# Weight-stationary blocks in 512-column matmuls: high weights against high and low activations at once, summed when the bank is emptied

## The chip, the cores and the metric

One Trainium2 chip, one of its cores. The metric is the device time of one execution in microseconds; a measurement is the median of several executions. A profiled execution also gives a trace of every instruction, with its start, its duration and what it waited for. The engines are TensorE (PE in the trace; its weight loads PEld), VectorE (DVE), ScalarE (ACT), GpSimd (POOL) and SyncE (SP), which issues the DMAs.

## The reference

Three transformer layers over 256 tokens of width 1024, batch 1, in float32, one after the other:

```
x = first_block(x, ...)      # convolutions + stick-breaking attention, then a feed-forward of 4096
return second_block(x, ...)  # layer 0: retention, gated conv feed-forward of 2816
                             # layer 1: differential attention, gated conv feed-forward of 2816

# the projections are all of this kind, x normalised before and residuals around:
p = h @ w_in                                # 1024 -> 2816 columns, cut into conv parts and q, k, v
x = x + square(relu(h2 @ w_ff1)) @ w_ff2
proj = xn @ a_w_in                          # retention: q, k, v, g
h = xn @ w_up ; hc = causal_conv3(h) ; (silu(hc_g) * hc_u) @ w_down
```

A first conv part goes into the sum as `y_a = a_b * conv3(a_c * a_h)`, a second through a causal convolution of 31 taps, a layer norm and a SiLU (`y_b`), and the attention as `y_c`; `[y_a, y_b, y_c] @ w_out` closes the first mixing.

## The kernel before, in words

Each float32 matrix product is made of float32r matmuls (one pass each) over split numbers: a weight unit of 128 x 1024 is loaded by DMA into `raw`, ACT copies it rounded into `hi`, DVE writes the rest into `lo`; activations are split in the same way into a high and a low half (`sx.hi`, `sx.lo`: eight blocks of 128 channels x 256 tokens). A product is then high x high + high x low + low x high, three matmuls into one PSUM bank (128 x 512 float32; there are eight banks).

There are three ways to walk a product. `wstat` (line 508) keeps 128 x 128 weights in the array and streams the 256 tokens: eight steps over the channels with three matmuls each, on half a bank, and the result has channels on the partitions. `xstat` and `xstat_tokens` keep activations in the array and stream 512 weight columns. `Down` (line 576) does the closing projections in the second way with an accumulator of two banks for each half of the tokens; it takes up the activations `y` one block of 128 channels at a time, and holds back the second token half of the last seven blocks until the first half is done.

The order of the instructions is planned. `Flow` (line 145) runs the kernel's generators against a clock of its own, with a cost for each operation, and hands each engine its operations in the order in which they come up there; each engine then has this order fixed. When several are ready, the lower priority number goes first: CHAIN, ATT, EVAC, SPLIT, IDLE, MAIN (line 236). On DVE and ACT that means attention chains, then the emptying of banks, then weight splits (which run ahead of TensorE by a ring of eight units), and last IDLE, which is the 31-tap convolution `conv_b` of the mix stage (line 719) on DVE. `Slots` hands out banks and buffers, first come first served.

The names that matter: in the mix stage `qk_evac` (833) copies q and k out of a bank, `conv_a` (849) takes three blocks, `MIX_KT` sets that the closing projection takes up blocks 4, 5, 6, 7, 0, 2, 3, 1, of which 2 and 3 come from `conv_b`. In the feed-forward `evac` (933) applies ReLU and square. In retention `rotate` (988) reads two blocks that lie in the two halves of one bank. In the conv stages (two of them, `conv_phase`, 1112) `gate` (1128) reads the gate block and the up block in the halves of one bank, convolves both (three taps: one ACT, two DVE operations each), multiplies and splits; four gates at the start (`early`, 1164) get their blocks by transposes, and `lagged` sets the closing step of block i five blocks behind its up. In the attention stage `evac` (1209) copies q and k.

Of the kernel before, what the change touches and what calls it, by code (L numbers as in the profile page):

```python
# [238 lines left out]
class Acts:  # L239


    def __init__(self, hi, lo):
        self.hi, self.lo = hi, lo
        self.reset()
# [13 lines left out]
def chain_kernel(ctx: ExitStack, tc: tile.TileContext, x_in, wpack, gains, chan, small_rows, consts, out):  # L258
# [153 lines left out]
    ch = cpool.tile([P, NCH], F32, tag="ch", name="ch")  # L412
    sx = Acts(cpool.tile([P, KD, S], F32R, tag="xh", name="xh"), cpool.tile([P, KD, S], F32R, tag="xl", name="xl"))

# [70 lines left out]
    def residual_post(t, acc, ready, g, hg):  # L485
# [20 lines left out]
        return [stt(p, x, h, r, x, ALU.mult, ALU.add) for x, h in zip(xs, hs)]  # L506

    def wstat(dst, w, sx):
        hi, lo = yield from take("ws", w)
        h3 = hi.rearrange("p (k c) -> p k c", k=KD)  # L510
        l3 = lo.rearrange("p (k c) -> p k c", k=KD)
        for k in range(KD):
            if k % 4 == 0:
                yield sx.ready[0][k // 4]
                yield sx.ready[1][k // 4]
            o = pe(MAIN, 358, [
                mm(dst, h3[:, k, :], sx.hi[:, k, :], k == 0, False),
                mm(dst, h3[:, k, :], sx.lo[:, k, :], False, False),
                mm(dst, l3[:, k, :], sx.hi[:, k, :], False, k == KD - 1)])
            yield o.end  # L520
        release(ring, o)
        return o
# [110 lines left out]
    def mix_phase(mp):  # L633
# [199 lines left out]
        def qk_evac(pp, o, dst):  # L833
            yield o
            yield act(EVAC, dst, pp[:, :S], AF.Copy)
            banks.put()

        for i in range(4):
            pr = []
            for what in range(2):  # L840
                pp = yield from banks.get()
                o = yield from wstat(pp[:, :S], "w_in", sx)
                d = yield from qks.get()
                pr.append((d, flow.spawn(qk_evac(pp, o, d))))
            flow.spawn(stick(i, pr))
            if i == V_AFTER:
                yield from xstat("w_in", sx, v_evac)

        def conv_a(c, banks3, o1, o2, o3):
            pc, ph, pb = banks3  # L850
            yield o1
            ac = mp.tile([P, S], F32, tag=f"ac{c}", name=nm("ac"))
            yield act(EVAC, ac, pc[:, :S], AF.Copy)
            banks.put()
            up = mp.tile([P, S + 2], F32, tag=f"up{c}", name=nm("up"))
            nc.gpsimd.memset(up[:, 0:2], 0.0)
            yield o2
            yield tt(EVAC, up[:, 2:], ph[:, :S], ac, ALU.mult)
            banks.put()
            yield consts_in  # L860
            ca = ac
            yield ts(EVAC, ca, up[:, 2:], ch[:, CA0 + 3 * c + 2:CA0 + 3 * c + 3], None, ALU.mult)
            for j in (1, 0):
                yield stt(EVAC, ca, up[:, j:j + S], ch[:, CA0 + 3 * c + j:CA0 + 3 * c + j + 1], ca, ALU.mult, ALU.add)
            yield o3
            yield tt(EVAC, ca, pb[:, :S], ca, ALU.mult)
            banks.put()
            yield from split_to(EVAC, yh[:, c, :], yl[:, c, :], ca)
            flow.fire(y_ready[c])

        for c in range(2):
            trio, ops = [], []
            evs = [Ev() for _ in range(3)]
            pc = yield from banks.get()
            o1 = yield from wstat(pc[:, :S], "w_in", sx)
            ph = yield from banks.get()
            o2 = yield from wstat(ph[:, :S], "w_in", sx)
            pb = yield from banks.get()
            o3 = yield from wstat(pb[:, :S], "w_in", sx)
            flow.spawn(conv_a(c, (pc, ph, pb), o1, o2, o3))  # L880
# [19 lines left out]
    def ff_phase(fp):  # L900
# [32 lines left out]
        def evac(pp, o, y):  # L933
            yield o
            rl = yield from rls.get()
            yield act(EVAC, rl, pp[:, :S], AF.Relu)
            banks.put()
            yield tt(EVAC, rl, rl, rl, ALU.mult)
            yield from split_to(EVAC, y[0], y[1], rl)
            rls.put()  # L940
# [16 lines left out]
        for what, i in lagged(NF, 8):  # L957
            if what == "up":
                pp = yield from banks.get()
                o = yield from wstat(pp[:, :S], w1, sx)  # L960
                y = yield from both.get()
                ys[i] = (y, flow.spawn(evac(pp, o, y)), both)
            else:
                yield from dn.step(*ys.pop(i))
# [8 lines left out]
    def ret_phase(rp):  # L973
# [9 lines left out]
        qs = [Slots(flow, 1, lambda w=w: rp.tile([P, 2, S], F32, tag=f"q{w}", name=nm("q"))) for w in range(2)]  # L983
        rots = Slots(flow, 1, lambda: [rp.tile([P, 2, S], F32, tag=f"rot{c}", name=nm("rot")) for c in "cs"])
        pds = Slots(flow, 1, lambda: [rp.tile([P, 384], d, tag=f"pd{c}", name=nm("pd")) for c, d in (("f", F32), ("h", F32R), ("l", F32R))])
        sgs = slots(rp, 2, [P, 512], F32, "sgl")

        def rotate(pp, o, dst):
            yield o
            for c in cops:  # L990
                yield c
            tcos, tsin = yield from rots.get()
            p3 = pp.rearrange("p (a c) -> p a c", a=2)
            a = tt(EVAC, tcos, p3, cosb.broadcast_to([P, 2, S]), ALU.mult)
            b = tt(EVAC, tsin, p3, sinb.broadcast_to([P, 2, S]), ALU.mult)
            yield a
            yield b
            banks.put()
            a = tt(EVAC, dst[:, 0, :], tcos[:, 0, :], tsin[:, 1, :], ALU.subtract)
            b = tt(EVAC, dst[:, 1, :], tsin[:, 0, :], tcos[:, 1, :], ALU.add)  # L1000
            yield a
            yield b
            rots.put()
# [60 lines left out]
        for h in range(RH):  # L1064
# [30 lines left out]
            for what in range(2):  # L1095
                pp = yield from banks.get()
                yield from wstat(pp[:, 0:S], "a_w_in_2", sx)
                o = yield from wstat(pp[:, S:2 * S], "a_w_in_2", sx)
                d = yield from qs[what].get()
                pr.append((d, flow.spawn(rotate(pp, o, d))))  # L1100
# [11 lines left out]
    def conv_phase(layer, fp, gain_ids, chain_of):  # L1112
# [3 lines left out]
        both = Slots(flow, TAIL + 2, lambda: (fhs.make(), fls.make()))  # L1116
        cvs = Slots(flow, 3, lambda: [fp.tile([P, S], F32, tag=f"cv{c}", name=nm("cv"), bufs=3) for c in range(2)])
        nat = fp.tile([P, 2, D], F32, tag="nat", name="nat")
        n_ready = [[Ev(), Ev()], [Ev(), Ev()]]
# [8 lines left out]
        def gate(pp, o_g, o_u, i, y, nat_i):  # L1128
            cg, cu = yield from cvs.get()
            ps_g, ps_u = pp[:, 0:S], pp[:, S:2 * S]  # L1130
            if nat_i is not None:
                for e in n_ready[0] + n_ready[1]:
                    yield e
                o_g, o_u = [tp(EVAC, [(d[:, t * P:(t + 1) * P], nat[:, t, c0 + nat_i * P:c0 + (nat_i + 1) * P]) for t in range(2)])
                            for d, c0 in ((ps_g, 0), (ps_u, 512))]
            yield o_g
            yield o_u
            a = flow.spawn(conv(EVAC, ps_g, cg, 0, i))
            b = flow.spawn(conv(EVAC, ps_u, cu, 1, i))
            yield a  # L1140
            o = act(EVAC, cg, cg, AF.Silu)
            yield b
            banks.put()
# [27 lines left out]
        for what, i in lagged(NF2, 4):  # L1171
            if what == "up":
                pp = yield from banks.get()
                o_g = yield from wstat(pp[:, 0:S], w_up, sx)
                o_u = yield from wstat(pp[:, S:2 * S], w_up, sx)
                y = yield from both.get()
                ys[i] = (y, flow.spawn(gate(pp, o_g, o_u, i, y, None)), both)
            else:
                yield from dn.step(*ys.pop(i))

    def diff_phase(dp, sb):
# [27 lines left out]
        def evac(pp, o, d, p):  # L1209
            yield o  # L1210
            yield act(p, d, pp[:, :S], AF.Copy)
            banks.put()
# [102 lines left out]
        for h in range(DH):  # L1315
            pr = []
            p = CHAIN + 0.5 if h >= DH - URGENT else ATT
            for what in range(2):
                pp = yield from banks.get()
                o = yield from wstat(pp[:, :S], "w_kv_2" if what == 0 else "b_w_q_2", sx if what == 0 else sb)  # L1320
                d = yield from qks[what].get()
# [21 lines left out]
    def main():  # L1343
# [6 lines left out]
        with tc.tile_pool(name="bresp", bufs=1, reuse_waits="tile") as bp:  # L1350
            sb = Acts(bp.tile([P, KD, S], F32R, tag="bh", name="bh"), bp.tile([P, KD, S], F32R, tag="bl", name="bl"))
            with tc.tile_pool(name="cf0p", bufs=1, reuse_waits="tile") as fp:
# [105 lines left out]
```

## Time and profile before

| | |
|---|---|
| median of 3 runs | 994.86 us (994.24 to 995.26) |
| profiled execution, its own time | 995.56 us |
| its span, first to last instruction | 993.8 us |
| mean granted TensorE clock | 0.998 of full speed |
| TensorE busy | 980.7 us (99%), 6108 matmuls |
| DVE busy | 689.3 us (69%) |
| ACT busy | 562.5 us (57%) |

How to read it: a matmul's row starts when it enters the array, and its modelled end overlaps the next one, so the pace is the distance between starts. All operations are recorded in one helper, so every row says L198, and groups are told apart by their tiles: `bank<-xh,hi` is a matmul that streams high activations against high weights. The 256-column groups are the blocks of `wstat`, the 512-column ones the other two ways. A DVE or ACT row's duration also overlaps its successor a little.

### The profile page before, as it was taken

How to read it: one execution, taken by the hardware profiler on the slowest of the kernel's cores; microseconds unless marked ns; L12 is line 12 of the kernel's file. 1: busy time of each engine (PE TensorE's matmuls, PEld its weight loads, DVE VectorE, ACT ScalarE, POOL GpSimd, SP SyncE). 2: the span in 40 equal slices, each digit the busy share in tenths (PEclk: the TensorE clock that was granted, in tenths of full speed). 3: DMA queues.
4: the chain of work that ended last, by engine and by line, in shares of the span. 5: the costliest groups of instructions: out<-in, count | busy, mean ns of one | idle time of the engine just before them, and what ended most of it. 6: DMA issues, size and time to landing. Idle time of an engine off the chain costs nothing.

```text
span 993.8 us, 15342 instructions
## 1 busy us (share of the span) xinstructions
PE 980.7 (99%) x6108; PEld 876.1 (88%) x6108; DVE 689.3 (69%) x1076; ACT 562.5 (57%) x952; POOL 30.2 (3%) x52
## 2 busy tenths in 40 slices
PE   7999999999999999999999999999999999999997
PEld 5899889999988989988889999997899789999996
DVE  5899775555558756665579666668777579776663
ACT  6654564444446444544567555556677767555551
POOL 1000000000000000000000000001000100000000
PEclk9999999999999999999999999999999999999999
DMA  8744455555436744554366555543733155655531
GB/s 300 257 133 176 179 212 187 195 173 207 171 128 228 264 164 147 178 188 174 123 219 250 185 192 173 209 169 135 266 148 134 54 199 205 236 182 177 184 107 43
DMA packets 28585, 180.14 MB, mean 181 GB/s; under 512 B 3168, under 2 KB 4448, under 8 KB 8672
## 3 DMA queue, kind: packets, MB, share of 16 engines
q1 hardware_dynamic: 28512, 179.14, 50.7%
q8 instruction: 48, 0.79, 0.3%
q14 instruction: 25, 0.20, 0.1%
HBM read 178.08 MB, written 1.05 MB: 180 GB/s over the span
## 4 chain that ended last, share of the span: by engine, by line
PE 92%; DVE 2%; ACT 2%; issue 2%; DMA 1%; POOL 1%; SPq 0%; DVEq 0%; POOLq 0%; ACTq 0%
PE bank L198 92%; ACT junk L198 1%; DVE lo L198 1%; DMA big<-gains 1%; POOL tiny L198 1%; DVE x L198 1%; DVE big L198 0%; ACT hi L198 0%; ACT L198 0%; DVE tiny L198 0%; ACT pe L198 0%; ACT aT L198 0%; DVE xl L198 0%; ACT dyh L198 0%; SPq L198 0%
## 5 line engine op out<-in xcount | busy, mean ns | idle before, releaser
L198 DVE TENSOR_TENSOR lo<-raw,hi 128x1024 fp32r<-128x1024 f32 (+1 forms) x344 | 393.7, 1153 | 129.7 <-ACT hi L198 128.5
L198 ACT ACTIVATE hi<-raw 128x1024 fp32r<-128x1024 f32 (+1 forms) x344 | 341.2, 1003 | 154.6 <-PE bank L198 138.9
L198 PE MATMUL bank<-xh,hi 128*128 128x256 f32 x1072 | 306.1, 286 | 0.0
L198 PE MATMUL bank<-xh,lo 128*128 128x256 f32 x1072 | 303.3, 283 | 0.0
L198 PE MATMUL bank<-xl,hi 128*128 128x256 f32 x1072 | 303.3, 283 | 0.0
L198 PEld LDWEIGHTS bank<-xh,hi 128*128 128x128 f32 x1072 | 205.4, 192 | 3.7 <-issue 1.0
L198 PEld LDWEIGHTS bank<-xl,hi 128*128 128x128 f32 x1072 | 205.4, 192 | 2.6
L198 PEld LDWEIGHTS bank<-xh,lo 128*128 128x128 f32 x1072 | 205.3, 191 | 0.0
L198 PE MATMUL bank<-hi,xh 128*128 128x512 f32 x288 | 114.1, 396 | 0.0
L198 PE MATMUL bank<-lo,xh 128*128 128x512 f32 x288 | 112.4, 390 | 0.2 <-DVE lo L198 0.2
L198 PE MATMUL bank<-hi,xl 128*128 128x512 f32 x288 | 112.5, 391 | 0.0
L198 DVE SCALAR_TENSOR_TENSOR cv<-bank,ch,cv 128x254 f32<-128x254 f32 (+1 forms) x176 | 72.5, 476 | 51.6 <-ACT cv L198 51.4
L198 PE MATMUL bank<-hi,fh 128*128 128x512 f32 x272 | 106.9, 393 | 0.0
L198 PE MATMUL bank<-lo,fh 128*128 128x512 f32 x272 | 106.5, 391 | 0.0
L198 PE MATMUL bank<-hi,fl 128*128 128x512 f32 x272 | 105.8, 389 | 0.0
L198 ACT ACTIVATE cv<-bank,ch 128x256 f32<-128x256 f32 x88 | 44.1, 561 | 61.4 <-PE bank L198 61.4
L198 PEld LDWEIGHTS bank<-hi,xl 128*128 128x128 f32 x288 | 54.0, 188 | 11.8 <-DVE xl L198 0.2
L198 PEld LDWEIGHTS bank<-lo,xh 128*128 128x128 f32 x288 | 54.2, 188 | 11.5 <-DVE lo L198 1.0
L198 PEld LDWEIGHTS bank<-hi,xh 128*128 128x128 f32 x288 | 54.1, 188 | 10.4
L198 PEld LDWEIGHTS bank<-hi,fl 128*128 128x128 f32 x272 | 51.1, 188 | 11.0
L198 PEld LDWEIGHTS bank<-hi,fh 128*128 128x128 f32 x272 | 51.3, 189 | 9.1
L198 PEld LDWEIGHTS bank<-lo,fh 128*128 128x128 f32 x272 | 51.3, 189 | 8.5
(167 smaller groups left out, 1039.8 us busy)
## 6 DMA issues: line engine op xcount, KB each, us to landing
raw<-wpack SPq DMA_DIRECT2D x155, 1024.0 KB, 4.8
big<-gains SPq DMA_DIRECT2D x12, 512.0 KB, 6.9
raw<-wpack SPq DMA_DIRECT2D x12, 512.0 KB, 6.9
x<-x SPq DMA_DIRECT2D x4, 256.0 KB, 6.1
out_dram<-x SPq DMA_DIRECT2D x4, 256.0 KB, 2.2
dec<-consts SPq DMA_DIRECT2D x4, 192.0 KB, 5.0
one<-consts SPq DMA_DIRECT2D x1, 384.0 KB, 6.3
ch<-chan SPq DMA_DIRECT2D x1, 213.5 KB, 5.9
```

What stands on the lines that cost most here:

```text
L198: fn(*a, **k)
```

## The change

The high and the low half of the activations become the two planes of one tile (`both`). In each step of `wstat` the high weights meet both planes in one 512-column matmul, which fills the whole bank: high x high in its first half, high x low in its second. The low weights meet the high activations in a 256-column matmul into the first half. A block so has two matmuls a step in place of three, and takes a whole bank. Whoever empties the bank has to add its halves: `join` copies the second half out by ACT and adds the first on DVE. Where two blocks shared a bank (`rotate`, `gate`), they now take two banks, and `rotate` and `gate` work on the joined copies in SBUF. The planned cost of a step goes from 358 to 347.

```diff
 class Acts:
-    def __init__(self, hi, lo):
-        self.hi, self.lo = hi, lo
+    def __init__(self, both):
+        self.both = both
+        self.hi, self.lo = both[:, 0], both[:, 1]
...
-    sx = Acts(cpool.tile([P, KD, S], F32R, tag="xh", name="xh"), cpool.tile([P, KD, S], F32R, tag="xl", name="xl"))
+    sx = Acts(cpool.tile([P, 2, KD, S], F32R, tag="xhl", name="xhl"))
...
+    def join(p, out, d):
+        yield act(p, out, d[:, S:], AF.Copy)
+        yield tt(p, out, d[:, :S], out, ALU.add)
+
     def wstat(dst, w, sx):
...
+        d2 = dst.rearrange("p (a c) -> p a c", a=2)
         for k in range(KD):
...
-            o = pe(MAIN, 358, [
-                mm(dst, h3[:, k, :], sx.hi[:, k, :], k == 0, False),
-                mm(dst, h3[:, k, :], sx.lo[:, k, :], False, False),
-                mm(dst, l3[:, k, :], sx.hi[:, k, :], False, k == KD - 1)])
+            o = pe(MAIN, 347, [
+                mm(d2, h3[:, k, :], sx.both[:, :, k, :], k == 0, False),
+                mm(dst[:, :S], l3[:, k, :], sx.hi[:, k, :], False, k == KD - 1)])
...
         def qk_evac(pp, o, dst):
             yield o
-            yield act(EVAC, dst, pp[:, :S], AF.Copy)
+            yield from join(EVAC, dst, pp)
...
         def conv_a(c, banks3, o1, o2, o3):
...
-            yield act(EVAC, ac, pc[:, :S], AF.Copy)
+            yield from join(EVAC, ac, pc)
             banks.put()
...
             yield o2
-            yield tt(EVAC, up[:, 2:], ph[:, :S], ac, ALU.mult)
+            hs = mp.tile([P, S], F32, tag=f"hs{c}", name=nm("hs"))
+            yield from join(EVAC, hs, ph)
             banks.put()
+            yield tt(EVAC, up[:, 2:], hs, ac, ALU.mult)
...
             yield o3
-            yield tt(EVAC, ca, pb[:, :S], ca, ALU.mult)
+            yield from join(EVAC, hs, pb)
             banks.put()
+            yield tt(EVAC, ca, hs, ca, ALU.mult)
...
-            yield act(EVAC, rl, pp[:, :S], AF.Relu)
+            yield from join(EVAC, rl, pp)
             banks.put()
-            yield tt(EVAC, rl, rl, rl, ALU.mult)
+            yield stt(EVAC, rl, rl, 0.0, rl, ALU.max, ALU.mult)
...
-            tcos, tsin = yield from rots.get()
-            p3 = pp.rearrange("p (a c) -> p a c", a=2)
+            tcos, tsin, p3 = yield from rots.get()
+            for j in [flow.spawn(join(EVAC, p3[:, n, :], pp[n])) for n in range(2)]:
+                yield j
+            banks.put(2)
...
-                pp = yield from banks.get()
-                yield from wstat(pp[:, 0:S], "a_w_in_2", sx)
-                o = yield from wstat(pp[:, S:2 * S], "a_w_in_2", sx)
+                pp = yield from banks.get(2)
+                yield from wstat(pp[0], "a_w_in_2", sx)
+                o = yield from wstat(pp[1], "a_w_in_2", sx)
...
+        sums = Slots(flow, 2, lambda: [fp.tile([P, S], F32, tag=f"sum{c}", name=nm("sum"), bufs=2) for c in range(2)])
...
         def gate(pp, o_g, o_u, i, y, nat_i):
             cg, cu = yield from cvs.get()
-            ps_g, ps_u = pp[:, 0:S], pp[:, S:2 * S]
             if nat_i is not None:
+                ps_g, ps_u = pp[:, 0:S], pp[:, S:2 * S]
...
-            yield o_g
-            yield o_u
+                yield o_g
+                yield o_u
+            else:
+                ps_g, ps_u = yield from sums.get()
+                yield o_g
+                yield from join(EVAC, ps_g, pp[0])
+                banks.put()
+                yield o_u
+                yield from join(EVAC, ps_u, pp[1])
+                banks.put()
...
-                pp = yield from banks.get()
-                o_g = yield from wstat(pp[:, 0:S], w_up, sx)
-                o_u = yield from wstat(pp[:, S:2 * S], w_up, sx)
+                pp = yield from banks.get(2)
+                o_g = yield from wstat(pp[0], w_up, sx)
+                o_u = yield from wstat(pp[1], w_up, sx)
...
         def evac(pp, o, d, p):
             yield o
-            yield act(p, d, pp[:, :S], AF.Copy)
+            yield from join(p, d, pp)
```

The diff is cut to its core; the other sites (the three blocks of `conv_a`, the feed-forward and the attention stage) pass the whole bank to `wstat` in the same way, and `gate` gives its `sums` back where it gave its bank back.

## Rows read from the trace of the kernel before

**Rows 1.** The page: busy time of TensorE and DVE (us, share of the span, instructions), and the chain of work that ended last by engine.

```profile
PE 980.7 (99%) x6108; PEld 876.1 (88%) x6108; DVE 689.3 (69%) x1076; ACT 562.5 (57%) x952; POOL 30.2 (3%) x52
...
PE 92%; DVE 2%; ACT 2%; issue 2%; DMA 1%; POOL 1%; SPq 0%; DVEq 0%; POOLq 0%; ACTq 0%
```

**Rows 2.** Busy time by stretch: length, then us (and instructions) of PE, PEld, DVE, ACT and POOL, the granted clock, the DMA share and GB/s. The stretches are the mix, the feed-forward and the first conv stage.

```profile
20.00:96.00 76.00, 75.64 (x538) 68.81 (x537) 72.89 (x122) 44.90 (x75) 1.19 (x3) 1.00 0.56 196
...
134.00:295.00 161.00, 160.54 (x983) 144.25 (x982) 93.48 (x118) 81.11 (x124) 1.48 (x2) 1.00 0.54 191
...
492.00:672.00 180.00, 180.00 (x1215) 166.92 (x1214) 132.29 (x211) 107.98 (x166) 1.94 (x2) 1.00 0.56 198
```

**Rows 3.** Groups of PE instructions: count, busy us, mean ns of one, idle time before. One matmul of each three of a block; the other two have groups of the same count.

```profile
L198 PE MATMUL bank<-xh,hi 128*128 128x256 f32 x1072 | 306.1, 286 | 0.0
...
L198 PE MATMUL bank<-bh,hi 128*128 128x256 f32 x64 | 18.3, 286 | 0.0
```

**Rows 4.** PE in order of time in the feed-forward (start us, duration us): the end of a block, the twelve matmuls of a closing step, the start of the next block. Between 199.83 and 202.23 lie nineteen rows of the same kind 0.12 apart.

```profile
199.83 0.28 PE L198 MATMUL bank<-xl,hi 128*128 128x256 f32 x1
...
202.23 0.40 PE L198 MATMUL bank<-hi,fh 128*128 128x512 f32 x1
202.46 0.40 PE L198 MATMUL bank<-lo,fh 128*128 128x512 f32 x1
202.70 0.39 PE L198 MATMUL bank<-hi,fl 128*128 128x512 f32 x1
...
204.97 0.28 PE L198 MATMUL bank<-xh,hi 128*128 128x256 f32 x1
205.09 0.28 PE L198 MATMUL bank<-xl,hi 128*128 128x256 f32 x1
```

**Rows 5.** PE in order of time in a run of 512-column matmuls of retention: the first and the last of 44 rows.

```profile
399.43 0.39 PE L198 MATMUL bank<-lo,xh 128*128 128x512 f32 x1
...
409.18 0.39 PE L198 MATMUL bank<-hi,xl 128*128 128x512 f32 x1
```

**Rows 6.** The instructions on the tile trib: duration ns least/median/most, first and last start. The moving operand is a 128-column block taken twice.

```profile
L198 PE MATMUL bank<-trib,identb x8: 272/278/283, 35.2 to 71.2; 128*128 128x256 bf16 x8
```

**Rows 7.** DVE's busy time by stretch in the mix stage (length, busy us and instructions, granted clock).

```profile
50.00:60.00 10.00, 10.00 (x22) 1.00 0.44 141
...
70.00:80.00 10.00, 10.00 (x18) 1.00 0.32 109
80.00:92.00 12.00, 12.00 (x25) 1.00 0.44 141
```

**Rows 8.** DVE in order of time at the end of the mix stage (start, duration): the last bank read of the first conv_a, splits, the last three operations of conv_b's taps (`cb<-gpad`), and the low half of conv_b's first result.

```profile
87.36 0.41 DVE L198 TENSOR_TENSOR ac<-bank,ac 128x256 f32<-128x256 f32 x1
87.69 1.20 DVE L198 TENSOR_TENSOR lo<-raw,hi 128x1024 fp32r<-128x1024 f32 x1
...
89.16 1.26 DVE L198 SCALAR_TENSOR_TENSOR cb<-gpad,ch,cb 128x256 f32<-128x256 f32 x3
90.35 1.21 DVE L198 TENSOR_TENSOR lo<-raw,hi 128x1024 fp32r<-128x1024 f32 x1
...
94.65 1.22 DVE L198 TENSOR_TENSOR lo<-raw,hi 128x1024 fp32r<-128x1024 f32 x1
...
98.03 0.41 DVE L198 TENSOR_TENSOR yl<-cb,yh 128x256 fp32r<-128x256 f32 x1
```

**Rows 9.** PE in order of time in the closing projection of the mix stage: the first and the third matmul of block 2 (conv_b's first result, high and low half).

```profile
100.92 0.39 PE L198 MATMUL bank<-hi,yh 128*128 128x512 f32 x1
...
101.38 0.39 PE L198 MATMUL bank<-hi,yl 128*128 128x512 f32 x1
```

**Rows 10.** PE by stretch at the start: length, busy us and instructions, granted clock.

```profile
8.00:10.00 2.00, 0.11 (x1) 0.87 1.02 380
10.00:12.00 2.00, 2.00 (x10) 0.50 1.03 417
12.00:14.00 2.00, 2.00 (x9) 0.77 1.04 422
```

**Rows 11.** PE in order of time at the start; in brackets the idle time before the instruction and what ended it.

```profile
9.89 1.11 PE L198 MATMUL bank<-ident,big 128*128 128x128 f32 x4 [2.58 <-DVE big L198]
```

**Rows 12.** Who waited for whom: us in total, times, longest us.

```profile
ACT hi L198 <- PE bank L198: 138.9, 134, 2.4
```

**Rows 13.** Groups by shape: a DVE operation on two 256-column operands and an ACT copy of 256 columns out of a bank; count, busy us, mean ns of one, idle before.

```profile
L198 DVE TENSOR_TENSOR rl<-rl 128x256 f32<-128x256 f32 x24 | 10.2, 425 | 24.3 <-ACT rl L198 24.3
...
L198 ACT ACTIVATE qk<-bank 128x256 f32<-128x256 f32 x8 | 3.1, 386 | 6.3 <-PE bank L198 6.3
```

**Rows 14.** The end of the first conv stage in order of time: the last gate's high half on ACT, and the first matmul that reads it on PE.

```profile
669.62 0.42 ACT L198 ACTIVATE fh<-cv 128x256 fp32r<-128x256 f32 x1 [1.38 <-DVE cv L198]
...
670.67 0.39 PE L198 MATMUL bank<-hi,fh 128*128 128x512 f32 x1
```

**Rows 15.** The end of the attention stage in order of time: the last head's q on ACT, and the first matmul on PE that reads its output.

```profile
771.35 0.42 ACT L198 ACTIVATE q<-bank 128x256 f32<-128x256 f32 x1
...
786.76 0.51 PE L198 MATMUL bank<-hi,dyh 128*128 128x512 f32 x1 [0.56 <-ACT dyh L198]
```

**Rows 16.** DVE in order of time at the start of the first conv stage: ten operations of the early gates merged.

```profile
520.44 4.13 DVE L198 SCALAR_TENSOR_TENSOR cv<-bank,ch,cv 128x255 f32<-128x255 f32 x10
```

More of the change, by code (lines that the diff above doesn't have):

```diff
@@ L841, in mix_phase @@
                 pp = yield from banks.get()
-                o = yield from wstat(pp[:, :S], "w_in", sx)
+                o = yield from wstat(pp, "w_in", sx)
                 d = yield from qks.get()
@@ L874, in mix_phase @@
             pc = yield from banks.get()
-            o1 = yield from wstat(pc[:, :S], "w_in", sx)
+            o1 = yield from wstat(pc, "w_in", sx)
             ph = yield from banks.get()
-            o2 = yield from wstat(ph[:, :S], "w_in", sx)
+            o2 = yield from wstat(ph, "w_in", sx)
             pb = yield from banks.get()
-            o3 = yield from wstat(pb[:, :S], "w_in", sx)
+            o3 = yield from wstat(pb, "w_in", sx)
             flow.spawn(conv_a(c, (pc, ph, pb), o1, o2, o3))
@@ L959, in ff_phase @@
                 pp = yield from banks.get()
-                o = yield from wstat(pp[:, :S], w1, sx)
+                o = yield from wstat(pp, w1, sx)
                 y = yield from both.get()
@@ L983, in ret_phase @@
         qs = [Slots(flow, 1, lambda w=w: rp.tile([P, 2, S], F32, tag=f"q{w}", name=nm("q"))) for w in range(2)]
-        rots = Slots(flow, 1, lambda: [rp.tile([P, 2, S], F32, tag=f"rot{c}", name=nm("rot")) for c in "cs"])
+        rots = Slots(flow, 1, lambda: [rp.tile([P, 2, S], F32, tag=f"rot{c}", name=nm("rot")) for c in "csq"])
         pds = Slots(flow, 1, lambda: [rp.tile([P, 384], d, tag=f"pd{c}", name=nm("pd")) for c, d in (("f", F32), ("h", F32R), ("l", F32R))])
@@ L997, in rotate @@
             yield b
-            banks.put()
             a = tt(EVAC, dst[:, 0, :], tcos[:, 0, :], tsin[:, 1, :], ALU.subtract)
@@ L1142, in gate @@
             yield b
-            banks.put()
+            if nat_i is not None:
+                banks.put()
+            else:
+                sums.put()
             yield o
@@ L1319, in diff_phase @@
                 pp = yield from banks.get()
-                o = yield from wstat(pp[:, :S], "w_kv_2" if what == 0 else "b_w_q_2", sx if what == 0 else sb)
+                o = yield from wstat(pp, "w_kv_2" if what == 0 else "b_w_q_2", sx if what == 0 else sb)
                 d = yield from qks[what].get()
@@ L1350, in main @@
         with tc.tile_pool(name="bresp", bufs=1, reuse_waits="tile") as bp:
-            sb = Acts(bp.tile([P, KD, S], F32R, tag="bh", name="bh"), bp.tile([P, KD, S], F32R, tag="bl", name="bl"))
+            sb = Acts(bp.tile([P, 2, KD, S], F32R, tag="bhl", name="bhl"))
             with tc.tile_pool(name="cf0p", bufs=1, reuse_waits="tile") as fp:
```

## The prediction

> **What bounds the kernel now.** I read first the busy shares and the chain of work that ended last: TensorE is busy 980.7 of 993.8 us and carries 92% of the chain, VectorE (DVE) is busy 69% of the time [rows 1]. So a nanosecond that TensorE is spared is a nanosecond of the end, as long as nothing new makes TensorE wait. The second view is the busy time by stage: TensorE has no hole in the mix stage (20 to 96 us), the feed-forward stage (134 to 295) or the first conv stage (492 to 672), and DVE has room in two of them (93 of 161, 132 of 180 us), but hardly any in the mix stage, 72.9 of 76 [rows 2]. Those are the two things to weigh: what TensorE saves per block, and whether the mix stage can pay for it on DVE.
>
> Third, the price of a matmul is read from start to start, not from its duration (a matmul row lasts 0.28 us or 0.39 us, since they overlap). Twenty matmuls of 256 columns lie between 199.83 and 202.23: 0.120 us each [rows 4]. Forty-three of 512 columns lie between 399.43 and 409.18: 0.2267 us each [rows 5]. The difference, 0.1067 us for 256 columns, is 256 columns at the 2.4 GHz that are granted there (clock 1.00 [rows 2]), so about 0.013 us of either is there once per matmul, whatever its width.
>
> **The change, part by part.**
>
> *Matmuls.* A step of a weight-stationary block is three 256-column matmuls, 3 x 0.120 = 0.360 us. It becomes one of 512 and one of 256: 0.227 + 0.120 = 0.347, so 0.013 us less. There are 1072 + 64 = 1136 steps [rows 3] (142 blocks of 8: 14 in mix, 24 in feed-forward, 16 in retention, 72 in the two conv stages, 16 in the attention stage). 1136 x 0.013 = **14.8 us less**. How a 512 and a 256 behave in turn is not in the trace; the nearest rows are the borders between the two widths. Behind a run of 256s the first 512s follow at 0.23 to 0.24 us [rows 4], and in front the first 256 behind 512s goes by in 0.12, by their starts 204.97 and 205.09 [rows 4]. So a step could cost as much as 0.236 + 0.120 = 0.356 (4.5 us saved in all) and, since starts are rounded to 0.01 and that 0.12 may be 0.11, as little as 0.337 (26 saved). I take 0.347: what one border loses the other gives back. The moving operand of the 512 is now two pieces of 256, the high and low activations, 8 KB apart in each partition. The only matmuls with a moving operand in two pieces are the eight that add the mask, 256 bf16 columns, and they last 0.278 us at the median [rows 6] against 0.286 of an ordinary 256 [rows 3]: no cost for a piece. I take none; the other bound is the second rival.
>
> One rule of the Trainium skill speaks against this saving. "TensorE: Matmul & The Clock Gate", section "Back-to-back issue gap", gives a warm matmul of N columns N/2.4 + 2.5 ns. By it the fixed part would be 2.5 ns and the change would save 1136 x 2.5 ns = 2.8 us, by that page an estimate; the trace disagrees with it here, with 120 and 226.7 ns where it has 109 and 216.
>
> *Joins.* Each of the 142 blocks now leaves the bank by an ACT copy of the second half and a DVE add of the first. In qk_evac, conv_a's first operand, the feed-forward and the attention evacuation the copy takes the place of one that was there; 92 copies are new (4 in conv_a, 16 in retention, 72 in conv), 0.386 us each as an ACT copy of 256 from a bank, 35.5 us of ACT. The 142 adds are all new: a DVE add of 256 lasts 0.425 [rows 13] and makes the next one wait 0.33 (starts 87.36 and 87.69 [rows 8]), 47 us of DVE. On average both are hidden: feed-forward DVE goes to 93 + 24 x 0.33 = 101 of 161, a conv stage to 132 + 36 x 0.33 = 144 of some 175 [rows 2]. Weights stay ahead: the weight split waits on ACT for 138.9 us until TensorE frees a ring slot [rows 12], so the splits, which the adds overtake in priority, have slack. An add waits for its copy, and behind it on DVE stand splits; the order is written out with the copy's time in it, so I cost that wait at nothing. Were this cover gone, each split behind it would be some 0.1 us late, out of a lead of many us.
>
> *Mix stage: where the cover is gone.* conv_b (62 DVE operations at the lowest priority) fills every hole of DVE: 10.00 of 10 us busy from 50 on, 12.00 of 12 from 80 to 92 [rows 7]. Its last three operations end at 90.42; after a chain of transposes and norm the low half of its first result is written by 98.03 + 0.41 = 98.44 [rows 8]. TensorE reads that result from 100.92 (the low half at 101.38) [rows 9]: a slack of 2.9 us. The change brings TensorE there 14 x 8 x 0.013 = 1.5 us sooner and puts 12 adds (8 of q and k, 3 of the first conv_a, 1 of the second) ahead of conv_b, 12 x 0.33 = 4.0 us. Stall: 4.0 + 1.5 - 2.9 = 2.6 us as the lower bound. The upper: conv_b, later, also falls behind work that came after its end so far, two splits (90.35 and 94.65, 1.2 us each [rows 8]) and the second conv_a, some 1.9 us of small operations with its own joins. Were all that done ahead of conv_b and not in the holes of the norm chain: 2.6 + 4.3 = 6.9. I take 5.5, as that work is released by TensorE's progress, which goes on while conv_b is late. So **5.5 us more**.
>
> *Clock.* Ahead of 9.89 us TensorE idled for 2.58 us [rows 11], and the granted clock then was 0.87, 0.50 and 0.77 in the three stretches of 2 us from 8 on [rows 10]: 2 x (0.13 + 0.50 + 0.23) = 1.7 us of full clock lost. A stall of 5 us can bring that; two small groups of transposes fall into it. 0 to 1.7, I take 1.0.
>
> *Ends of the conv stages.* The last gate's high half is written by 669.62 + 0.42 = 670.04, and TensorE reads it at 670.67 [rows 14]: 0.6 us of slack. The up half's join adds 0.39 + 0.42 and some 0.1 of handing over, 0.9 (the gate half's lies earlier, beside the up matmuls). 0.3 us late, twice: 0.6. If a split (1.2) gets between, 1.5 each; 0 if the planned order finds room.
>
> *Starts of the conv stages.* An up block now takes two banks. Four early gates hold four, two ups four, and the down accumulators two and two more: 12 for 8, against 10 so far. The early gates keep DVE full (ten conv operations in one run from 520.44 [rows 16]), so the second accumulator may wait for a gate or a join: 0 to 1 us each, I take 0.2, so 0.4. In retention two banks for q and two for k stand beside the values' at most four, so I take nothing there; in the steady conv loop four banks are free and an up's pair is released while the next one runs.
>
> *End of the attention stage.* TensorE already idles 0.56 us for the last head's output [rows 15]; its q, copied at 771.35 [rows 15], now takes an add more, 0.42 with the handing over 0.5. I take 0.5 (0 to 1).
>
> **Sum**: -14.8 + 5.5 + 1.0 + 0.6 + 0.4 + 0.5 = -6.8 us. The profiled execution took 995.56 us with a span of 993.8; it becomes 988.8. The median of the runs is 0.7 below the profiled one: 994.86 - 6.8 = 988.1, so 988.
>
> **The rivals.**
>
> *The mix stage hides it.* If conv_b gives way without a stall, 5.5 and 1.0 drop out: -13.3, 981.6 us. Against it speaks DVE's full 12.00 of 12 us [rows 7]; for it, only that the chain behind conv_b holds filler work that would be gone. 0.12.
>
> *The 512s stay at the border price.* If each 512 behind a 256 costs 0.233 as at 202.23 [rows 4], a step is 0.353, 8.0 us saved, 8.0 spent: 994.9, no change. For it speaks that every 512 now stands behind a 256. Against it, that the 256 behind a 512 starts earlier. 0.11.
>
> *Slower: the split moving operand.* A 512 read in two pieces 8 KB apart costs 0.013 or more above the 0.227, so a step is 0.360 again, nothing is saved and 8.0 is spent: 1002.9. It decides from 6 ns a matmul (1136 x 6 = 6.8). Against it: the mask matmuls [rows 6]; for it: they are bf16 and repeat one block, so no row shows two float pieces. 0.08.
>
> *Slower: the fixed part is not saved.* If what is above streaming belongs to the columns and not to the matmul, a 512 takes 2 x 0.120 and a step stays at 0.360: 1002.9 again. The 43 matmuls at 0.2267 speak against it [rows 5]. 0.02. The rule of the Trainium skill named above ("TensorE: Matmul & The Clock Gate", "Back-to-back issue gap") would leave 2.8 us of saving and end near 1000.
>
> *More bank waits than I see* in retention or conv, 4 us and over: 992 to 995. 0.05.
>
> **How the numbers follow.** The forecast has 0.62. The range goes from the first rival (981) over the forecast to the second (995); beyond it lie the slower rivals and the best price of a step, about 0.2. What a measurement of this kernel can tell from no change is 0.2%, 2 us. Faster: 0.62 + 0.12 + 0.03 of the last rival = 0.77. Same: 0.11 + 0.02 = 0.13. Slower: 0.10.
>
> **What would show it.** In the profile after: starts of a 512 and a 256 in turn 0.347 us apart (0.340 to 0.360 separates the rivals); one hole of TensorE near 100 us, ahead of the down matmuls that read conv_b's result, of 3 to 7 us, with a granted clock of 0.5 behind it; holes under 1.5 us at the ends of the conv stages; no hole in feed-forward and retention. I am wrong if that hole is missing (faster), or if 512s are at 0.233 and above (no gain), or if TensorE waits for banks in the conv loop.

## The result, and the profile after

The changed kernel takes 998.0 us at the median of 8 runs (996.69 to 998.67), the kernel before 994.96 beside it (8 runs, 994.24 to 995.67): ratio 1.0027, 95% interval 1.0016 to 1.0038. So it is slower by 3.0 us, clear of the measurement's uncertainty, where 988.0 was forecast, and it lies outside the range of 981 to 995.

The profiled execution took 996.76 us with a span of 995.0, 1.2 us more than the profiled one of before. It is one of three low runs among the eight (996.69 to 996.76; the other five lie between 997.86 and 998.67). What follows is read from it; why the median lies another 1.2 higher is taken up with experiment 6.

Busy time on the page (us, share of the span, instructions), and the chain of work that ended last by engine, against [rows 1]:

```profile
PE 976.3 (98%) x4972; PEld 817.1 (82%) x4972; DVE 742.4 (75%) x1218; ACT 589.1 (59%) x1044; POOL 31.0 (3%) x52
...
PE 86%; DVE 8%; issue 2%; ACT 2%; DMA 1%; POOL 1%; SPq 0%; DVEq 0%; POOLq 0%; ACTq 0%
```

TensorE executes 1136 matmuls fewer and is busy only 4.4 us less. DVE has 53 us more to do, ACT 27. And the chain spends 8% of the span on DVE where it spent 2%: something new waits for DVE. Where, the chain in order of time tells (start us, us, what):

```profile
22.58 20.93 PE bank L198 x120
...
46.50 1.20 DVE lo L198
...
70.99 1.98 DVE cb L198 x5
...
98.76 0.41 DVE cb L198
```

Between 46 and 99 us, in the mix stage, every one of the 86 pieces is DVE's or a gap between two of them. In the kernel before the chain has a single piece there, 702 matmuls of TensorE:

```profile
23.20 110.60 PE bank L198 x702
```

DVE has become the bound of the mix stage.

**By stage.** In us of the profiled execution, each from the end of the one above to the start of the last matmul of the stage named, with two exceptions. The first begins with the first transposes of the mix stage, at 23.20 before and 22.58 after. The feed-forward begins with its own first transposes (123.13 before, 129.59 after), 7.9 us behind the end of the row above in every kernel. Beside before and after stand four of the experiments below:

| stretch, up to | before | after | by width (2) | mix as before (3) | both (7) | no adds in mix (5) |
|---|---|---|---|---|---|---|
| closing projection of mix, first low half | 69.51 | 67.81 | 68.11 | 69.53 | 69.53 | 67.91 |
| the same, last low half | 22.51 | **31.30** | 32.32 | 22.50 | 22.51 | 23.13 |
| feed-forward | 174.79 | 173.77 | 172.22 | 173.76 | 172.22 | 173.75 |
| retention | 196.50 | 195.73 | 195.38 | 195.62 | 195.42 | 195.62 |
| first conv stage | 189.46 | 187.43 | 186.13 | 187.47 | 186.15 | 187.37 |
| attention, last low half of its output | 115.04 | 115.65 | 115.64 | 114.35 | 115.54 | 115.80 |
| second conv stage | 188.31 | 186.27 | 184.95 | 186.27 | 184.89 | 186.24 |

Three things stand in the column of after: the stages of blocks gain, but less than forecast; the closing projection of the mix stage loses 8.8 us at one place; attention loses 0.6. The closing projection, PE in order of time (start, duration; in brackets the idle time before and what ended it), against [rows 9]:

```profile
97.67 0.39 PE L198 MATMUL bank<-lo,yh 128*128 128x512 f32 x1
97.90 0.39 PE L198 MATMUL bank<-hi,yl 128*128 128x512 f32 x1
99.31 0.85 PE L198 MATMUL bank<-ident,cb 128*128 128x128 f32 x4 [1.02 <-DVE cb L198]
102.36 1.33 PE L198 MATMUL bank<-ident,gpad 128*128 128x128 f32 x4 [2.20 <-DVE gpad L198]
105.73 0.80 PE L198 MATMUL bank<-hi,yh 128*128 128x512 f32 x1 [2.04 <-ACT yh L198]
106.33 0.63 PE L198 MATMUL bank<-lo,yh 128*128 128x512 f32 x1
...
108.46 0.63 PE L198 MATMUL bank<-hi,yh 128*128 128x512 f32 x1
108.89 0.47 PE L198 MATMUL bank<-lo,yh 128*128 128x512 f32 x1
109.20 0.40 PE L198 MATMUL bank<-hi,yl 128*128 128x512 f32 x1
109.43 0.40 PE L198 MATMUL bank<-hi,yh 128*128 128x512 f32 x1
```

Between 98.13 and 105.73 TensorE has only the eight transposes of conv_b's result to do. Behind the hole matmuls last 0.63 instead of 0.39, and nine of them take 3.70 us (105.73 to 109.43) where nine at 0.227 take 2.04: 1.7 us more. PE by stretch (length, busy us and instructions, granted clock) has the clock at 0.50, 1.2 GHz, there, as it was at the start of the program [rows 10]:

```profile
104.00:106.00 2.00, 0.27 (x1) 0.50 0.00 0
106.00:108.00 2.00, 2.00 (x5) 0.50 0.00 0
108.00:110.00 2.00, 2.00 (x8) 0.74 0.00 0
110.00:112.00 2.00, 2.00 (x11) 1.00 0.00 0
```

What the hole waits for, DVE in order of time, against [rows 8]:

```profile
92.77 0.42 DVE L198 TENSOR_TENSOR hs<-bank,hs 128x256 f32<-128x256 f32 x1
93.11 0.48 DVE L198 SCALAR_TENSOR_TENSOR cb<-gpad,ch,cb 128x256 f32<-128x256 f32 x1
93.50 0.42 DVE L198 TENSOR_TENSOR up<-hs,ac 128x256 f32<-128x256 f32 x1
...
94.49 1.22 DVE L198 TENSOR_TENSOR lo<-raw,hi 128x1024 fp32r<-128x1024 f32 x1
...
98.67 0.89 DVE L198 SCALAR_TENSOR_TENSOR cb<-gpad,ch,cb 128x256 f32<-128x256 f32 x2
...
105.71 0.76 DVE L198 TENSOR_TENSOR yl<-cb,yh 128x256 fp32r<-128x256 f32 x2
```

conv_b's last tap ends at 99.56, where it ended at 90.42: 9.1 us later. ACT's high half of its result releases TensorE at 105.73, and DVE's low half follows from 105.71 on. Between its taps stand joins (`hs<-bank,hs`), the second conv_a (`up<-hs,ac`) and splits that in the kernel before came behind it.

The price of a step, PE in order of time, one block of the feed-forward stage (205.24 to 208.05), against [rows 4]:

```profile
205.24 0.39 PE L198 MATMUL bank<-xhl,hi 128*128 128x512 f32 x1
205.46 0.28 PE L198 MATMUL bank<-xhl,lo 128*128 128x256 f32 x1
205.58 0.40 PE L198 MATMUL bank<-xhl,hi 128*128 128x512 f32 x1
205.81 0.28 PE L198 MATMUL bank<-xhl,lo 128*128 128x256 f32 x1
205.93 0.40 PE L198 MATMUL bank<-xhl,hi 128*128 128x512 f32 x1
206.17 0.28 PE L198 MATMUL bank<-xhl,lo 128*128 128x256 f32 x1
...
208.05 0.40 PE L198 MATMUL bank<-hi,fh 128*128 128x512 f32 x1
```

Eight steps in 2.81 us are 0.351 a step. The median is 2.810 us for a block behind a closing step and 2.830 (0.354) for one behind another block; before it was 2.873 and 2.880 (0.359 and 0.360). The 512s take 0.22 to 0.24 from start to start and the 256s 0.11 to 0.12, whichever of the two comes next.

### The profile page after: what moved, and what is told of

It reads as the page before. It is cut to its first block, busy times and chain, and to the rows that moved or that the text cites. A ratio compares the mean times of both kernels' runs of the same rounds, so it can differ in the third digit from the quotient of the medians.

```text
span 995.0 us, 13319 instructions
## 1 busy us (share of the span) xinstructions
PE 976.3 (98%) x4972; PEld 817.1 (82%) x4972; DVE 742.4 (75%) x1218; ACT 589.1 (59%) x1044; POOL 31.0 (3%) x52
## 3 DMA queue, kind: packets, MB, share of 16 engines
HBM read 178.08 MB, written 1.05 MB: 180 GB/s over the span
## 4 chain that ended last, share of the span: by engine, by line
PE 86%; DVE 8%; issue 2%; ACT 2%; DMA 1%; POOL 1%; SPq 0%; DVEq 0%; POOLq 0%; ACTq 0%
PE bank L198 86%; DVE lo L198 3%; DVE cb L198 2%; ACT junk L198 1%; DMA raw<-wpack 1%; POOL tiny L198 1%; DVE x L198 1%; ACT hi L198 0%; DVE ac L198 0%; DVE big L198 0%; DVE run L198 0%; DVE beta L198 0%; ACT L198 0%; DVE xhl L198 0%; DVE tiny L198 0%
## 5 line engine op out<-in xcount | busy, mean ns | idle before, releaser
L198 PE MATMUL bank<-xhl,hi 128*128 128x512 f32 x1072 | 384.7, 400 | 0.0
L198 PE MATMUL bank<-xhl,lo 128*128 128x256 f32 x1072 | 300.4, 280 | 0.0
L198 PEld LDWEIGHTS bank<-xhl,hi 128*128 128x128 f32 x1072 | 201.4, 188 | 47.2 <-issue 0.6
L198 PEld LDWEIGHTS bank<-xhl,lo 128*128 128x128 f32 x1072 | 202.4, 189 | 2.6
L198 PE MATMUL bank<-hi,xhl 128*128 128x512 f32 x576 | 185.1, 394 | 0.0
L198 PEld LDWEIGHTS bank<-hi,xhl 128*128 128x128 f32 x576 | 108.2, 188 | 22.4 <-DVE xhl L198 0.3
L198 PE MATMUL bank<-lo,xhl 128*128 128x512 f32 x288 | 112.3, 390 | 0.2 <-DVE lo L198 0.2
L198 PEld LDWEIGHTS bank<-lo,xhl 128*128 128x128 f32 x288 | 54.3, 188 | 11.4 <-DVE lo L198 0.7
L198 DVE SCALAR_TENSOR_TENSOR cv<-sum,ch,cv 128x255 f32<-128x255 f32 (+1 forms) x144 | 60.5, 475 | 1.0 <-ACT cv L198 1.0
L198 PEld LDWEIGHTS bank<-hi,fl 128*128 128x128 f32 x272 | 51.1, 188 | 11.6
L198 ACT ACTIVATE cv<-sum,ch 128x256 f32<-128x256 f32 x72 | 39.6, 589 | 3.9 <-DVE sum L198 3.9
```

Of the source, the lines that this page charges most:

```text
L198: fn(*a, **k)
```

## The experiments

Each was measured against runs of the kernel before on the same chip: 994.77 us for experiments 1 to 4, 994.73 for 5 to 7. All start from the changed kernel. Its 998.0 us comes from the series of the result and was not measured again beside them, so a difference to it is sure only to about a microsecond; each ratio is to the kernel before in the same series.

**1. The two planes side by side.** The activations' high and low halves of a step become neighbours, so that the 512 reads one piece. Theory A says that the change of width between neighbours costs, theory B that the two pieces do.

```
-    sx = Acts(cpool.tile([P, 2, KD, S], ...))
+    sx = Acts(cpool.tile([P, KD, 2, S], ...))      # same for sb
-    mm(d2, h3[:, k, :], sx.both[:, :, k, :], ...)
+    mm(dst, h3[:, k, :], sx.both[:, k].rearrange("p a c -> p (a c)"), ...)
```

> The changed kernel, with the two planes of the activations laid so that the high and the low 256 of a block lie side by side (tile of 8 blocks x 2 planes x 256): the 512-column matmul reads one piece of 512 and not two of 256. In the changed kernel a step takes 0.236 + 0.117 = 0.353 us where 0.347 was forecast. Theory A (it is the change of width from one matmul to the next that costs): nothing moves, the starts stay 0.236 and 0.117 us apart, time within 1 us of the changed kernel's 998.0. Theory B (the operand in two pieces costs 6 to 9 ns a matmul): 512s fall to 0.227, 1136 x 6 ns = 6.8 us less, near 991.

997.19 us (7 runs, 995.29 to 998.35), ratio 1.0025 (1.0014 to 1.0036). The starts are those of the changed kernel (PE in order of time):

```profile
205.62 0.39 PE L198 MATMUL bank<-xhl,hi 128*128 128x512 f32 x1
205.85 0.28 PE L198 MATMUL bank<-xhl,lo 128*128 128x256 f32 x1
205.96 0.40 PE L198 MATMUL bank<-xhl,hi 128*128 128x512 f32 x1
206.19 0.28 PE L198 MATMUL bank<-xhl,lo 128*128 128x256 f32 x1
206.31 0.40 PE L198 MATMUL bank<-xhl,hi 128*128 128x512 f32 x1
```

B falls: one piece or two, a step takes 0.35.

**2. Ordered by width.** The same sixteen matmuls of a block, the eight 512s first, then the eight 256s.

```
 for k in range(KD):
-    o = pe(MAIN, 347, [mm(d2, h3[:, k, :], sx.both[:, :, k, :], ...), mm(dst[:, :S], l3[:, k, :], sx.hi[:, k, :], ...)])
+    o = pe(MAIN, 227, [mm(d2, h3[:, k, :], sx.both[:, :, k, :], ...)])
+    yield o.end
+for k in range(KD):
+    o = pe(MAIN, 120, [mm(dst[:, :S], l3[:, k, :], sx.hi[:, k, :], ...)])
```

> The changed kernel, with the sixteen matmuls of a block ordered by width: eight of 512 columns (high weights), then eight of 256 (low weights). Same operands, two pieces, same joins. Theory A (the change of width costs): 512s fall to 0.227 and 256s stay at 0.120 but for the first few behind a border, some 0.02 us a border, so a block is 8 x 0.347 + 0.02 against 8 x 0.353: 142 x 0.03 to 0.05 = 4 to 6 us less, 992 to 994. Theory B (two pieces cost): 512s stay at 0.236 throughout, time 998.

991.88 us (6 runs, 989.91 to 993.43), ratio 0.9969 (0.9957 to 0.998). PE in order of time, rows of one kind joined (from the start of the first):

```profile
204.94 0.39 PE L198 MATMUL bank<-hi,fl 128*128 128x512 f32 x1
205.16 1.98 PE L198 MATMUL bank<-xhl,hi 128*128 128x512 f32 x8
206.97 1.11 PE L198 MATMUL bank<-xhl,lo 128*128 128x256 f32 x8
207.93 0.40 PE L198 MATMUL bank<-hi,fh 128*128 128x512 f32 x1
```

The eight 512s take 1.81 us (0.226 each), the eight 256s 0.96 (0.120), the block 2.77: 0.346 a step, and 0.349 at the median behind another block, whose 256s make the first few 512s dearer again. The order of the widths alone is worth 6.1 us by the medians and 5.8 by the ratios, where 4 to 6 were expected; in the profiles the four stretches without a hole take 4.5 us less. Theory A holds, and theory B falls again: the operand is still in two pieces. It is not that high and low weights alternate, either: in the kernel before they alternate in 256s alone, at an even 0.120 [rows 4].

**3. The mix stage as before.** Its 14 blocks go back to three 256s a step and to the old evacuations; all else stays changed.

```
-    o1 = yield from wstat(pc, "w_in", sx)
+    o1 = yield from wstat3(pc[:, :S], "w_in", sx)   # the block of before, planned at 360 a step (358 before); the same for the others
-    yield from join(EVAC, ac, pc)
+    yield act(EVAC, ac, pc[:, :S], AF.Copy)         # and the other evacuations of before
```

> The changed kernel, with the fourteen blocks of the mix stage alone put back to three 256-column matmuls a step and to their old evacuations without a join. Theory (the joins' DVE work delays the convolution on DVE, and TensorE waits for it from 98.1 to 105.7 us and then runs at half clock to 109): hole and half clock vanish, some 6.8 + 1.6 us back, less 112 steps x 0.007 = 0.8: 7.6 us less, near 990.4. Rival (the hole comes from TensorE's being early, or from another engine's order, and not from the joins): a hole of 2 us or more stays ahead of the down matmuls that read the convolution's result, 995 or above.

989.84 us (5 runs, 988.8 to 990.77), ratio 0.9951 (0.9938 to 0.9963). The hole is gone and the closing projection is back at 22.50 us, as the theory had it: the change of the mix stage alone costs 8.2 us by the medians, net of what its blocks save, and 7.1 by the two rows of the mix stage in the table (8.8 less 1.7).

**4. The attention stage as before, too.** Experiment 3, and the blocks of the attention stage go back as well.

```
-    yield from join(p, d, pp)
+    yield act(p, d, pp[:, :S], AF.Copy)
-    o = yield from wstat(pp, "w_kv_2" if what == 0 else "b_w_q_2", ...)
+    o = yield from wstat3(pp[:, :S], "w_kv_2" if what == 0 else "b_w_q_2", ...)
```

> As the run with the mix stage put back, with the sixteen blocks of the attention stage put back as well. Theory (each head there is one chain of small operations, and the joins of q and k make the last head late by the 1.8 us that TensorE waits at 785.8, with a half clock behind it of some 1.5 us): 1.8 + 1.5 - 128 x 0.007 = 2.4 us less than that run, near 988. Rival (the last head is late because TensorE reaches it sooner, by other stages' gains or by chance of the planned order): the hole of about 1.8 us stays and the time is 0 to 1 us above that run.

988.95 us (5 runs, 988.28 to 989.56), ratio 0.9944 (0.993 to 0.9958). The longer wait is gone; what is left is the 0.56 us of before [rows 15], on PE in order of time:

```profile
780.46 0.58 PE L198 MATMUL bank<-ident,o 128*128 128x128 f32 x2
781.61 0.50 PE L198 MATMUL bank<-hi,dyh 128*128 128x512 f32 x1 [0.56 <-ACT dyh L198]
```

From the start of the last q matmul to the last head's transposes (`ident,o`) it is 15.20 us here and 16.66 in experiment 3. So the joins make the last head's chain 1.5 us longer; the wait is not just TensorE's coming earlier.

But the stage takes 115.28 us, 0.9 more than with the wait in experiment 3 (114.35). By the starts in the two traces TensorE idles 0.95 us less in the stage (1.28 against 2.23), while the matmuls of its 16 blocks, put back, take 1.95 more (48.23 against 46.28, 15 ns a step where the theory had 7). There was no half clock to win back: in experiment 3 the clock is 1.00 behind the wait. The median is 0.9 below experiment 3, less than the theory expected and within the spread of both. So the wait is the joins', as the theory said; it costs about what it idles, and the blocks of this stage earn more than the theory gave them.

**5. The adds left out in the mix stage.** TensorE's work is the changed kernel's; the evacuation copies the first half and doesn't add the second. The products of high weights and low activations of these 14 blocks are thereby missing from the result.

```
-    yield from join(EVAC, dst, pp)
+    yield from half(EVAC, dst, pp)        # half: act(p, out, d[:, :S], AF.Copy); the same for ac, hs, hs
```

> The changed kernel, with the DVE add of every join in the mix stage left out (fourteen adds; the copy takes the first half of the bank, so the high x low products of these blocks are missing from the result). The matmuls, 512 and 256, and the ACT copies stay. Theory (the DVE time of the adds, which goes ahead of the low-priority convolution, makes the hole): the convolution ends as early as in the kernel before, no hole before the block that reads it, no half clock; 6.8 + 1.6 us back, near 989.5. Rival (the hole comes from the new matmul form, by its earlier arrival, or from the copies): a hole of 2 us or more stays, 993 or above.

988.04 us (5 runs, 987.68 to 988.76), ratio 0.9936 (0.9923 to 0.9948). conv_b's last tap on DVE, and block 2 on PE, each in order of time:

```profile
90.11 0.48 DVE L198 SCALAR_TENSOR_TENSOR cb<-gpad,ch,cb 128x256 f32<-128x256 f32 x1
```

```profile
98.72 0.39 PE L198 MATMUL bank<-hi,yl 128*128 128x512 f32 x1
98.95 0.43 PE L198 MATMUL bank<-hi,yh 128*128 128x512 f32 x1
```

conv_b ends at 90.59, 9.0 us earlier than in the changed kernel, and TensorE goes on without a hole. It is the adds on DVE that make the hole, with what falls ahead of conv_b because of them, and neither the new matmuls nor the banks: fourteen adds of 0.33 are 4.6 us of the 9.0.

**6. The hole filled.** 24 matmuls of 512 columns on a tile of zeros stand ahead of block 2 in the closing projection, into a bank that nobody reads.

```
+    if k == 2:
+        b = yield from banks.get()
+        for _ in range(24):
+            o = pe(MAIN, 227, [mm(b, warm[:, 0:P], warm, True, True)])
+            yield o.end
+        yield o
+        banks.put()
```

> The changed kernel, with 24 matmuls of zeros (512 columns, 5.4 us at full clock) put into TensorE's queue ahead of the down matmuls that wait for the convolution's result, so that TensorE works in the hole. Theory (behind the hole the clock is halved for some 8 matmuls at 0.43 us where 0.227 is the pace, 1.6 us): the granted clock stays at 1.00 behind the hole and 1.6 us come back, near 996.4. Rival (the clock behind the hole costs nothing that shows, or the zeros themselves delay the convolution's transposes): 998 or above.

994.64 us (11 runs, 993.77 to 996.61), ratio 1.0002 (0.9993 to 1.001). PE by stretch:

```profile
106.00:108.00 2.00, 1.91 (x8) 1.00 0.00 0
108.00:110.00 2.00, 2.00 (x10) 1.00 0.00 0
```

The clock stays full behind the hole, and the closing projection takes 30.25 us, 1.05 less. Nine matmuls behind the hole take 2.19 us (106.09 to 108.28) where they took 3.70, so 1.5 come back; but the transposes of conv_b's result stand behind zeros, and block 2 starts 0.45 later, counted from the start of this projection's first low half. Another 1.3 is in the attention stage, 114.36 here against 115.65: together 2.35 us, nearly the 2.4 between the two profiled executions and the 2.5 between the two ratios. The medians lie 3.4 apart. In the attention stage TensorE idles in the changed kernel as well, and the clock fell behind it (PE in order of time, then by stretch):

```profile
787.56 0.59 PE L198 MATMUL bank<-ident,o 128*128 128x128 f32 x2 [1.61 <-ACT o L198]
788.71 0.80 PE L198 MATMUL bank<-hi,dyh 128*128 128x512 f32 x1 [0.56 <-ACT dyh L198]
```

```profile
789.00:791.00 2.00, 2.00 (x5) 0.50 0.00 0
```

In this experiment's profile the clock there is 1.00, and in that of experiment 3 too, where the same kernel text stands (PE by stretch, experiment 6, then 3):

```profile
787.00:789.00 2.00, 1.44 (x7) 1.00 0.00 0
...
782.00:784.00 2.00, 2.00 (x9) 1.00 0.00 0
```

So the fall in the attention stage is one that some executions have and others not; the profiles of experiments 1, 2, 5 and 7 have it. That it explains why the changed kernel's median lies above its profile is not shown, and the mean granted clock, which is on record for every execution, speaks against it. It orders the executions of experiment 2 (0.995 at 989.91 us, 0.990 at 993.43), but not those of the changed kernel (0.991 at 996.69, 0.993 at 998.15) or of experiment 1 (0.994 at 995.29 and at 998.35).

**7. Ordered by width, the mix stage as before.** The edits of experiments 2 and 3 together, and no other:

```
-    o = pe(MAIN, 347, [mm(d2, ...), mm(dst[:, :S], ...)])
+    o = pe(MAIN, 227, [mm(d2, ...)])                 # one loop over k
+    o = pe(MAIN, 120, [mm(dst[:, :S], ...)])         # and a second one behind it
-    o1 = yield from wstat(pc, "w_in", sx)
+    o1 = yield from wstat3(pc[:, :S], "w_in", sx)    # mix stage, with its old evacuations
```

> Both findings together: the mix stage's blocks as in the kernel before (three 256-column matmuls, no join), all other blocks by width (eight of 512, then eight of 256, joins). Theory: a block by width takes 2.766 to 2.793 us where the alternating one takes 2.810 to 2.830 and the old one 2.873 to 2.880; 128 blocks x 0.04 = 5.1 us less than the run with the mix stage put back (989.84), near 984.7, 1% under the kernel before. Rival (the earlier TensorE runs into the next limit: the last head of the attention stage or the ends of the conv stages open new holes): 987 to 990.

984.37 us (4 runs, 983.14 to 985.63), ratio 0.9893 (0.9878 to 0.9909): 10.4 us faster than the kernel before and 13.6 faster than the change. As expected, its gain is close to the two of the experiments added: 998.0 - 6.1 - 8.2 = 983.7. The wait in the attention stage is left in it, in its profile with a clock of 0.50 behind it:

```profile
777.63 0.59 PE L198 MATMUL bank<-ident,o 128*128 128x128 f32 x2 [1.20 <-ACT o L198]
```

## Why the prediction was wrong

**The failed step: the price of a step.** "I take 0.347: what one border loses the other gives back." It does not. In the four stretches without a hole (feed-forward, retention and both conv stages, 896 steps) the changed kernel takes 1.02 + 0.77 + 2.03 + 2.04 = 5.86 us less: 6.5 ns a step, not 13, and 5.9 us where 11.6 stood. Ordered by width the same stretches gain 2.57 + 1.12 + 3.33 + 3.36 = 10.4 us, 11.6 ns a step: the 13 ns of fixed part per matmul were read rightly from the two runs [rows 4, 5], and most of them are saved as long as neighbours have the same width.

The rows of the border were there, too [rows 4], but they were read one matmul deep. By the medians of the borders in the trace of the kernel before (50 of the one kind, 58 of the other), the first five 512s behind 256s take 233, 236, 228, 233 and 231 ns against 227 in a run, 26 more in all; the first two 256s behind 512s take 114 and 119 against 120, 7 less. The first of each do add up to 0.347, which the forecast took; the extra behind them was left out. Where every neighbour differs, as in the changed kernel, the two come to 237 and 117 at the mean, 0.353 a step. It is the second rival, the 512s at the border price, that names this size (0.353, from 0.233 and 0.120); it had a chance of 0.11. The third rival, the split operand, fell with experiment 1.

In the other two stages, where small matmuls interrupt the blocks, the price of a step came near the forecast: by the starts in the traces, without idle time, the blocks' matmuls take 1.35 us less over the 112 steps of the mix stage (41.60 to 40.25) and 1.87 less over the 128 of attention (48.18 to 46.31), 12 and 15 ns a step. By width they take no less (40.26 and 46.24 in experiment 2). Why was not followed up.

**The mix stage: mechanism right, size too small.** The hole is where it was forecast, ahead of block 2, for the reason given, with a clock of 0.50 behind it. The stretch lost 8.8 us where 5.5 + 1.0 stood: 1.7 of clock and 7.1 of stall. The terms: conv_b's end is 9.1 us later; its way to the low half's start is 1.5 shorter, with less other DVE work in between (6.1 us, 99.56 to 105.71, against 7.6 [rows 8]); TensorE reaches the closing projection 2.3 earlier (90.39 against 92.71); the old slack was 2.9. 9.1 - 1.5 + 2.3 - 2.9 = 7.0. So the upper bound of 6.9, which counted in the splits and the second conv_a that overtake conv_b, was the better reading; 5.5 took something off it on the plea that TensorE goes on while conv_b is late, and no row stood for that. That the bound fits to 0.1 is luck in part: it had conv_b 8.3 later (9.1) and TensorE 1.5 sooner (2.3), and the shorter way of 1.5, which it did not have, offsets both. Experiments 3 and 5 show the cause. The deeper point is in the chain of after: DVE is not late at one place, it bounds the stage from 46 us on, so what comes ahead of conv_b's end is paid.

**What came as forecast, and attention, which did not.** Joins are hidden elsewhere: no idle time of TensorE behind the blocks of feed-forward, retention and conv, and none at the ends and starts of the conv stages, for which 1.0 had been set aside. The end of attention has the wait that was named, but its price of 0.5 was too low: at full clock (experiment 3) TensorE idles 2.23 us in the stage against 1.05 before, 1.2 more, and the stage is 0.7 us shorter than before only because the blocks' matmuls take 1.9 less. In the profile of after the half clock behind the wait costs another 1.3, and the stage is 0.6 longer.

**The sum again**, by the profiled executions: forecast -6.8; the price of a step in the four stretches without a hole +5.8 (5.9 for 11.6); the ends and starts of the conv stages, which lie in these stretches, -1.0 (nothing for 1.0); the closing projection of mix +2.3 (8.8 for 6.5); attention +1.8 (0.6 longer, where 128 x 0.013 less 0.5 made it 1.2 shorter); the start of the program and the first stretch of mix -0.9 (0.62 and 1.70 gained, where 112 x 0.013 = 1.5 stood). That makes +1.2, as measured. The first transposes of mix start between 21.57 and 23.20 us in the nine profiles, so the 0.62 is within what the start varies.

**What stays open.** No row shows why a change of width costs TensorE about 7 ns a step; the runs show only that the order decides it. The width goes together with the part of the bank that is written (512s the whole, 256s the first half), and no run separates the two. And the distance of the changed kernel's median to its profiled execution, 1.2 us, is not explained.

## What to carry to other kernels

Price an instruction in the sequence in which it will stand: matmuls of two widths in turn cost more than the same matmuls in two runs, so put the wide ones of a block first and the narrow ones behind. Where borders between the widths are all that the trace shows, read them more than one matmul deep: here the extra ran on over five. An engine that looks 96% busy with low-priority filler has no room at all if that filler has a deadline: work added there is paid by whoever waits for the filler, and the work that overtakes it counts as well. So change the stages that have room, and leave the one that doesn't (experiment 7 does both).

## What the runs showed of the hardware

- Widths in turn: by the medians of starts, behind a closing step, the 512s of a block take 227, 233, 241, 236, 233, 241, 236 and 233 ns, and the 256s 113, 117, 120, 113, 117, 120, 113 and 117; behind another block both go on in the same cycle of three. Ordered by width, behind the 256s of the block ahead, the 512s take 233, 236, 228, 233 and 231, then 227, and the 256s 113, 119, then 120.
- A moving operand in two pieces 8 KB apart costs nothing that shows (997.19 against 998.0 us, the same starts).
- A pause of TensorE can cost its clock or not: in the attention stage a wait of 1.2 to 1.6 us, two transposes and another 0.56 were followed by 0.50 in five profiles (the changed kernel, experiments 1, 2, 5 and 7) and by 1.00 in two (experiments 3 and 6). The 7.6 us with eight transposes cost 1.7 us of clock, and none when 24 matmuls of zeros stood in front.
